# Issue order at a decoder block's two layer norms and at the joining of its seven-product banks

## The chip, the core and the metric

The kernel runs on one core of one Trainium2 chip. The time is the device time of one launch in microseconds (us). TensorE (PE in the profile; its weight loads are PEld) multiplies, VectorE (DVE) and ScalarE (ACT) do elementwise work, GpSimd (POOL) does very little and issues a few DMAs, SyncE (SP) issues the other DMAs. Lower is better.

## What is computed

One decoder block on 256 tokens of width 2048, in float32. Only its second half touches the change:

```python
mix = token_mixers(x, ...)                # ends in merged @ w_out
x = layer_norm(ALPHA * x + mix, ln1_g, ln1_b)
h = gelu(causal_dwconv(x @ w_gate, conv_w, conv_b)) * (x @ w_up)
x = layer_norm(ALPHA * x + h @ w_down, ln2_g, ln2_b)
x = x + sigmoid(x @ w_ple_gate) * (p @ w_ple_proj)
```

`w_out` and `w_ple_gate` are 2048 x 2048, `w_gate` and `w_up` 2048 x 5632, `w_down` 5632 x 2048, `w_ple_proj` 256 x 2048.

## The kernel before

**Split operands.** Each float32 operand is split into a rounded part `hi` and the rest `lo`; a product is hi times hi, hi times lo and lo times hi. Tokens form two halves, t = 0 and 1, of 128.

**Units.** Weights come in 284 units of 128 x 2048, used in a fixed order: 120 to 135 are `w_out`, 136 to 223 alternate gate and up, 224 to 267 are `w_down` (22 for each half of its output columns), 268 to 283 the last gate. `unit()` (line 179) hands out the next unit and first calls `prep()` (line 158) until the units up to two ahead are prepared. A prep, for each half h of the unit, loads `raw` by SyncE's queue (a ring of four half-unit tiles), copies it to `hi` on ScalarE (line 170, the helper of line 107) and subtracts on VectorE for `lo` (line 171). The `hi` and `lo` tiles are six each, that is three units.

**Order of the work.** The program is traced in Python order; a scheduler then orders each engine's instructions by priority and readiness in its own model of time. `tc.high_priority(n)` raises the priority of what is traced in it. `tc.keep_in_program_order(ins)` pins an instruction behind the one traced last before it on the same engine (an order of issue, with no semaphore). `tc.manual_schedule(engines=...)` keeps an engine to the traced order. SyncE is under it all along; TensorE only in `end1`.

**The down projection and its joining.** `residual()` (line 921) runs the residual projections in two halves of output columns through `x_half()` (line 324). Most units are multiplied directly into four PSUM banks. Some units of the down projection (`DNW`; nine in the first half, eight in the second) use seven products in place of eight, in `seven()` (line 284). Four of these go to extra banks p1, p5, p7 and p6; after the last such unit `joined()` (line 937) adds them to the residual `z`: ScalarE copies p1 to `ju` (line 107), VectorE does `z = ALPHA * z + p1` (line 943) and then a chain of additions (lines 943 and 948). All have the priority `P_STAT`, the highest.

**First layer norm (`end1`, line 1020).** TensorE's order is by hand: the last two units of `w_out` for token half 0 and then 1 (`tail_mm`; each call is six matmuls of 512 columns), mixed with the projection of `p` (`proj(k, t)`, six matmuls; its results go through `put`, a ScalarE copy and a store by GpSimd's queue), with turns, and with the first three gate and up units. `stat` makes mean and scale; `norm(g)` normalizes one of four blocks of 512 columns, on VectorE (lines 889 and 891) for g of 0 and 2 and on ScalarE (line 894) for the others; `turn(g)` transposes that block by four matmuls of 128 columns into one of two `mx` banks (line 901), from which the engines make `x1T`: for g of 1 and 3 in four pieces `lny` by turns on ScalarE and VectorE (lines 911 and 913), then a hi copy and a subtraction (line 916). `LN_ORDER` takes the blocks as 1, 0, 3, 2. `phase0(i)` multiplies unit 136 + i with token half 0 (16 matmuls of 256 columns, line 250), which needs only `hi` parts; `phase1(j)` does half 1 and all `lo` parts of the three units in four slices.

**Second layer norm (`ln_out`, line 836).** It does the same steps into `x2T`, called by `done2` for each token half when its columns are done; before half 1, `ple_proj` traces 24 matmuls of the projection. Here the scheduler orders TensorE too. Norms are on VectorE for g = 0 (line 849), else on ScalarE (line 852); transposes are line 855, the four pieces of each block lines 862 and 864, the subtraction 867. The following `x_half` for the gate starts with two units whose matmuls are traced for t = 0 and then for t = 1 (12 matmuls a unit and half).

Of the kernel before, what the change touches and what calls it, by code (L numbers as in the profile page):

```python
# [9 lines left out]
F32 = mybir.dt.float32  # L10
# [36 lines left out]
DNW = (DNP, DNP[:-1])  # L47
WH = 1152
# [7 lines left out]
def tile_block(ctx: ExitStack, tc: tile.TileContext, wu, wfv, wpp, xT_in, x_in, pT_in, wlr,  # L56
# [66 lines left out]
    sums, half = {}, {}  # L123
# [34 lines left out]
    def prep():  # L158
# [6 lines left out]
        for h in range(2):  # L165
# [5 lines left out]
            nc.vector.tensor_tensor(lo, raw, hi.bitcast(F32), ALU.subtract)  # L171
# [7 lines left out]
    def unit():  # L179
        u = n_used[0]  # L180
        n_used[0] += 1
        while n_prep[0] < min(NU, u + 3):
            prep()
        for v in (u, u + 1):
            if v in half:
                split_seven(v)
        return ready.pop(u)
# [136 lines left out]
    def x_half(name, act, K, evac, pulls=0, head=0, tail=0, mid=None, done=None, end=None,  # L324
               fine=False, ws=(), joined=None):
# [15 lines left out]
        for t in range(2):  # L341
            for i, w in enumerate(us):
                mm(i, w, (t,))
# [492 lines left out]
    def ln_out(zs, stats, t, act_out, cg, cb, nm, prio):  # L836
# [3 lines left out]
        with tc.high_priority(P_STAT):  # L840
            nc.vector.bn_aggr(mv[:, 0:2], stats[t])
            nc.vector.tensor_scalar(mv[:, 2:3], mv[:, 1:2], LN_EPS, None, ALU.add)
            nc.gpsimd.tensor_tensor(mv[:, 3:4], mv[:, 2:3], mhalf, ALU.pow)
            nc.vector.tensor_scalar(mv[:, 4:5], mv[:, 0:1], -1.0, mv[:, 3:4], ALU.mult, ALU.mult)
        with tc.high_priority(prio):
            for g in range(4):
                zc = z[:, g * 512:g * 512 + 512]
# [3 lines left out]
                else:  # L851
                    nc.scalar.activation(zc, zc, AF.Identity, scale=mv[:, 3:4], bias=mv[:, 4:5])
                pt = mxtile(f"pt{nm}{t}{g}")
# [15 lines left out]

    def ln_steps(zs, stats, t, act_out, gb_, cg, cb, nm):  # L870
# [13 lines left out]
        def norm(g):  # L884
            e = slice(g * 512, g * 512 + 512)
            zc = z[:, e]
            with tc.high_priority(P_LN1[t]):
                if g in AFF_DVE:
                    nc.vector.scalar_tensor_tensor(zc, zc, mv[:, 0:1], gb_[0][:, e],
                                                   ALU.subtract, ALU.mult)  # L890
                    nc.vector.scalar_tensor_tensor(zc, zc, mv[:, 3:4], gb_[1][:, e],
                                                   ALU.mult, ALU.add)
                else:
                    nc.scalar.activation(zc, zc, AF.Identity, scale=mv[:, 3:4], bias=mv[:, 4:5])
# [26 lines left out]
    def residual(name, act, K, zs, stats, mid, done=None, end=None, ws=((), ())):  # L921

        for nh in range(2):
# [13 lines left out]
            def joined(ms, zp=zp):  # L937
# [12 lines left out]
                with tc.high_priority(P_STAT):  # L950
                    copy(u, p1)

                onto(0, 0, p1)
# [47 lines left out]
    def ple_proj(half, w, pTs):  # L1001
        banks = [[[mmtile(f"pp{half}{t}{c}")] for c in range(2)] for t in range(2)]
        for k in range(2):
            o = slice(k * 1024, k * 1024 + 1024)
# [307 lines left out]
```

## Time and profile before

| | us |
|---|---|
| median of 3 runs | 1664.32 (1663.75 to 1664.76) |
| the profiled execution | 1663.05 |
| its span, first to last instruction | 1661.3 |
| TensorE busy with matmuls | 1650.9 |
| VectorE busy | 1193.2 |
| ScalarE busy | 865.4 |

Matmuls are pipelined, and the profile models their ends: a matmul's shown duration overlaps the next one's. Where TensorE's time matters, distances from start to start are read. A bracket at the end of a timeline row is the engine's idle time before it and what ended it. Line numbers (L171) are those of the kernel before. Arrows read out <- in, by the program's tile names with numbers left out, so `hi<-raw` stands for every unit.

### The profile page before, as it was taken

To read this page: it belongs to the slowest core of one execution; us is meant where nothing else is said; L and a number is where in the kernel's file an instruction comes from. 1 tells how busy PE (TensorE), PEld (TensorE's weight loads), DVE (VectorE), ACT (ScalarE), POOL (GpSimd) and SP (SyncE) were. 2 spreads that over 40 slices of the span, in tenths; PEclk is the share of its full clock that TensorE was granted. 3 is DMA by queue.
4 is the path that set the end of the run, shared out by engine and by line. 5 is a ranking of instruction groups with operands and counts; after the bars stand their busy time and mean duration, and the time that the engine had idled before them with its cause. 6 is when DMAs were issued, how large, how long until landed. Compare 5 with 4: busy or idle time off the path is not lost.

```text
span 1661.3 us, 24083 instructions
## 1 busy us (share of the span) xinstructions
PE 1650.9 (99%) x8984; PEld 1432.3 (86%) x8984; DVE 1193.2 (72%) x1751; ACT 865.4 (52%) x1245; POOL 62.8 (4%) x175
## 2 busy tenths in 40 slices
PE   9999999999999999999999999999999999999998
PEld 8988888888888888888888888888888888888787
DVE  6666658768756657775677777777777788887874
ACT  6745445445555544544465555555555555454733
POOL 0000000000000000000010000000000011010000
PEclk9999999999999999999999999999999999999999
DMA  7665555555555555667746666666666667695554
GB/s 295 232 201 183 165 188 181 177 179 177 184 178 174 173 189 194 194 195 283 235 150 209 231 232 205 206 211 205 205 209 205 202 246 271 223 345 208 183 192 168
DMA packets 95588, 343.87 MB, mean 207 GB/s; under 512 B 11064, under 2 KB 12736, under 8 KB 94064
## 3 DMA queue, kind: packets, MB, share of 16 engines
q1 hardware_dynamic: 90528, 324.51, 58.3%
q0 software_dynamic: 4944, 17.84, 2.8%
q8 instruction: 70, 1.15, 0.3%
q14 instruction: 46, 0.38, 0.1%
HBM read 332.33 MB, written 9.97 MB: 206 GB/s over the span
## 4 chain that ended last, share of the span: by engine, by line
PE 94%; DVE 2%; DMA 2%; ACT 1%; issue 1%; SPq 0%; POOL 0%; DVEq 0%; ACTq 0%
PE psu L237 9%; PE psg L237 9%; PE psm L237 7%; PE dn L281 7%; PE gr L281 5%; PE gv L281 5%; PE wo L281 5%; PE psu L239 5%; PE psg L239 5%; PE pg L281 4%; PE psm L239 4%; PE psa L237 3%; PE fv L426 2%; PE psfq L237 2%; PE psfk L237 2%; PE psq L237 2%
## 5 line engine op out<-in xcount | busy, mean ns | idle before, releaser
L107 ACT ACTIVATE hi<-raw 128x1024 fp32r<-128x1024 f32 (+1 forms) x568 | 593.0, 1047 | 629.2 <-issue 217.0
L171 DVE TENSOR_TENSOR lo<-raw,hi 128x1024 fp32r<-128x1024 f32 x534 | 653.1, 1225 | 358.1 <-ACT hi L107 357.1
L237 PE MATMUL psu<-x1T,hi 128*128 128x512 f32 x688 | 236.0, 389 | 0.0
L237 PE MATMUL psg<-x1T,hi 128*128 128x512 f32 x672 | 230.5, 389 | 0.0
L239 PE MATMUL psu<-x1T,lo 128*128 128x256 f32 x688 | 190.0, 276 | 0.0
L239 PE MATMUL psg<-x1T,lo 128*128 128x256 f32 x672 | 185.5, 276 | 0.0
L237 PE MATMUL psm<-xT,hi 128*128 128x512 f32 x512 | 175.8, 391 | 0.0
L237 PEld LDWEIGHTS psu<-x1T,hi 128*128 128x128 f32 x688 | 129.2, 188 | 26.7
L237 PEld LDWEIGHTS psg<-x1T,hi 128*128 128x128 f32 x672 | 126.2, 188 | 26.1
L239 PE MATMUL psm<-xT,lo 128*128 128x256 f32 x512 | 141.5, 276 | 0.0
L239 PEld LDWEIGHTS psu<-x1T,lo 128*128 128x128 f32 x688 | 129.1, 188 | 0.0
L239 PEld LDWEIGHTS psg<-x1T,lo 128*128 128x128 f32 x672 | 126.2, 188 | 0.0
L281 PE MATMUL dn<-hi,hT 128*128 128x512 f32 x432 | 121.4, 389 | 0.0
L237 PEld LDWEIGHTS psm<-xT,hi 128*128 128x128 f32 x512 | 96.2, 188 | 19.8
L239 PEld LDWEIGHTS psm<-xT,lo 128*128 128x128 f32 x512 | 96.2, 188 | 0.1
L281 PEld LDWEIGHTS dn<-hi,hT 128*128 128x128 f32 x432 | 81.0, 188 | 16.8 <-ACT hi L107 0.2
L237 PE MATMUL psa<-oT,hi 128*128 128x512 f32 x256 | 87.8, 389 | 0.0
L281 PE MATMUL gv<-hi,xT 128*128 128x512 f32 x256 | 72.3, 394 | 0.0
L281 PE MATMUL gr<-hi,xT 128*128 128x512 f32 x256 | 72.2, 394 | 0.0
L239 PE MATMUL psa<-oT,lo 128*128 128x256 f32 x256 | 70.7, 276 | 0.0
L281 PE MATMUL wo<-hi,mT 128*128 128x512 f32 x256 | 70.2, 390 | 0.0
L281 PE MATMUL dn<-lo,hT 128*128 128x512 f32 x216 | 68.9, 391 | 0.6 <-DVE lo L171 0.5
(300 smaller groups left out, 2806.2 us busy)
## 6 DMA issues: line engine op xcount, KB each, us to landing
raw<-in_wu_dram SPq DMA_DIRECT2D x568, 512.0 KB, 4.7
fvraw<-in_wfv_dram SPq DMA_DIRECT2D x14, 524.0 KB, 7.9
hi<-hsd POOLq DMA_DIRECT2D x17, 256.0 KB, 5.1
lo<-hsd POOLq DMA_DIRECT2D x17, 256.0 KB, 5.3
lnb<-in_lng_dram SPq DMA_DIRECT2D x4, 1024.0 KB, 9.0
hsd<-hsh POOLq DMA_DIRECT2D x9, 256.0 KB, 5.7
hsd<-hsl POOLq DMA_DIRECT2D x9, 256.0 KB, 5.5
z<-in_x_dram SPq DMA_DIRECT2D x2, 1024.0 KB, 8.5
```

The costliest lines, as they stand in the source:

```text
L107: nc.scalar.activation(o, i, AF.Copy, bias=0.0, scale=scale)
L171: nc.vector.tensor_tensor(lo, raw, hi.bitcast(F32), ALU.subtract)
L237: nc.tensor.matmul(ps, lhsT=hi[i // 8 if hoff == 0 else 0][:, w0 % 1024:w0 % 1024 + P], rhs=a[:, kt % 4, :], start=first and i == 0, stop= ...
L239: nc.tensor.matmul(ps[:, 256:512], lhsT=lo[i // 8 if hoff == 0 else 0][:, w0 % 1024:w0 % 1024 + P], rhs=a[:, kt % 4, 0:256], start=False, ...
L281: nc.tensor.matmul(bs[j][:, 0:m], lhsT=x, rhs=v[:, o:o + m], start=first and i == 0, stop=last and i == 2)
L426: nc.tensor.matmul(fbk[t][c][:, 0:n], lhsT=x, rhs=w[:, o:o + n], start=kt == 0 and i == 0, stop=kt == 15 and i == 2)
```

## The change

It alters the order in which instructions are issued.

- **Joining:** ScalarE's copy of p1 and VectorE's first addition are pinned behind what was traced before them on their engines; the last of this are hi copies and lo subtractions of the two units already asked for.
- **First border:** all four groups of `tail_mm` for half 1 come before the first turn, and the projection's groups shift between the turns. Half 1's norms, the projection's copies and the lo parts of units 137 and 138 (`LATE_LO`) are pinned behind half 0's last turn and then placed one by one between half 1's turns. `unit(3 - i)` asks for no further units in these phases.
- **Second border:** `ln_out` becomes `ln_parts`, which gives the same three steps as functions, and TensorE's order is written out from the last two dn units (`end2`) to the first two units of the gate (`begin3`). The lo parts of units 270 and 271 (`PIN_LO`) are pinned behind what was traced before them on VectorE.

```diff
@@ -45,6 +45,8 @@
 DNW = (DNP, DNP[:-1])
+LATE_LO = (137, 138)
+PIN_LO = (270, 271)
 WH = 1152
@@ -120,7 +122,7 @@
-    sums, half = {}, {}
+    sums, half, later = {}, {}, {}
@@ -168,7 +170,16 @@
             lo = w_tile("lo", F32R, f"lo{u}_{h}", u)
-            nc.vector.tensor_tensor(lo, raw, hi.bitcast(F32), ALU.subtract)
+            def rest(lo=lo, raw=raw, hi=hi):
+                return nc.vector.tensor_tensor(lo, raw, hi.bitcast(F32), ALU.subtract)
+            if u in LATE_LO:
+                later.setdefault(u, []).append(rest)
+            elif u in PIN_LO:
+                tc.keep_in_program_order(rest())
+            else:
+                rest()
             his.append(hi)
@@ -176,10 +187,10 @@
-    def unit():
+    def unit(ahead=3):
         u = n_used[0]
         n_used[0] += 1
-        while n_prep[0] < min(NU, u + 3):
+        while n_prep[0] < min(NU, u + ahead):
             prep()
@@ -322,7 +333,7 @@
     def x_half(name, act, K, evac, pulls=0, head=0, tail=0, mid=None, done=None, end=None,
-               fine=False, ws=(), joined=None):
+               fine=False, ws=(), joined=None, begin=None):
@@ -338,9 +349,12 @@
         us = [unit() for _ in range(head)]
-        for t in range(2):
-            for i, w in enumerate(us):
-                mm(i, w, (t,))
+        if begin is not None:
+            begin(lambda i, t: mm(i, us[i], (t,)))
+        else:
+            for t in range(2):
+                for i, w in enumerate(us):
+                    mm(i, w, (t,))
         for i in range(head, n - tail):
@@ -833,23 +847,31 @@
-    def ln_out(zs, stats, t, act_out, cg, cb, nm, prio):
+    def ln_parts(zs, stats, t, act_out, cg, cb, nm, prio):
...
         mv = sm.tile([P, 8], F32, tag="mv", name="mv")
-        with tc.high_priority(P_STAT):
-            nc.vector.bn_aggr(mv[:, 0:2], stats[t])
-            nc.vector.tensor_scalar(mv[:, 2:3], mv[:, 1:2], LN_EPS, None, ALU.add)
-            nc.gpsimd.tensor_tensor(mv[:, 3:4], mv[:, 2:3], mhalf, ALU.pow)
-            nc.vector.tensor_scalar(mv[:, 4:5], mv[:, 0:1], -1.0, mv[:, 3:4], ALU.mult, ALU.mult)
-        with tc.high_priority(prio):
-            for g in range(4):
-                zc = z[:, g * 512:g * 512 + 512]
+        def stat():
+            with tc.high_priority(P_STAT):
+                nc.vector.bn_aggr(mv[:, 0:2], stats[t])
+                nc.vector.tensor_scalar(mv[:, 2:3], mv[:, 1:2], LN_EPS, None, ALU.add)
+                nc.gpsimd.tensor_tensor(mv[:, 3:4], mv[:, 2:3], mhalf, ALU.pow)
+                nc.vector.tensor_scalar(mv[:, 4:5], mv[:, 0:1], -1.0, mv[:, 3:4],
+                                        ALU.mult, ALU.mult)
+        def norm(g):
+            zc = z[:, g * 512:g * 512 + 512]
+            with tc.high_priority(prio):
                 if g in ZN_DVE:
...
                     nc.scalar.activation(zc, zc, AF.Identity, scale=mv[:, 3:4], bias=mv[:, 4:5])
+        def turn(g):
+            zc = z[:, g * 512:g * 512 + 512]
+            with tc.high_priority(prio):
                 pt = mxtile(f"pt{nm}{t}{g}")
@@ -867,6 +889,8 @@
+        return stat, norm, turn
     def ln_steps(zs, stats, t, act_out, gb_, cg, cb, nm):
@@ -881,17 +905,18 @@
-        def norm(g):
+        def norm(g, keep=lambda ins: None):
             e = slice(g * 512, g * 512 + 512)
...
                 if g in AFF_DVE:
-                    nc.vector.scalar_tensor_tensor(zc, zc, mv[:, 0:1], gb_[0][:, e],
-                                                   ALU.subtract, ALU.mult)
+                    keep(nc.vector.scalar_tensor_tensor(zc, zc, mv[:, 0:1], gb_[0][:, e],
+                                                        ALU.subtract, ALU.mult))
                     nc.vector.scalar_tensor_tensor(zc, zc, mv[:, 3:4], gb_[1][:, e],
...
                 else:
-                    nc.scalar.activation(zc, zc, AF.Identity, scale=mv[:, 3:4], bias=mv[:, 4:5])
+                    keep(nc.scalar.activation(zc, zc, AF.Identity, scale=mv[:, 3:4],
+                                              bias=mv[:, 4:5]))
@@ -948,9 +973,10 @@
                 with tc.high_priority(P_STAT):
-                    copy(u, p1)
-                onto(0, 0, p1)
+                    tc.keep_in_program_order(nc.scalar.activation(u, p1, AF.Copy, bias=0.0,
+                                                                  scale=1.0))
+                    tc.keep_in_program_order(nc.vector.scalar_tensor_tensor(
+                        zp(0, 0), zp(0, 0), ALPHA, p1, ALU.mult, ALU.add))
                 plus(u, u, p6)
@@ -998,13 +1024,6 @@
-    def ple_proj(half, w, pTs):
-        banks = [[[mmtile(f"pp{half}{t}{c}")] for c in range(2)] for t in range(2)]
-        for k in range(2):
-            o = slice(k * 1024, k * 1024 + 1024)
-            x_mm(banks, (w[0][:, o], w[1][:, o]), pTs[k], (0, 1), k == 0, k == 1)
-        return banks
     z1 = [s8([P, 2048], name=f"z1{t}") for t in range(2)]
@@ -1033,13 +1052,14 @@
                     o = t2("ppo")
-                    copy(o, pb[t][c][0])
+                    tc.keep_in_program_order(nc.scalar.activation(
+                        o, pb[t][c][0], AF.Copy, bias=0.0, scale=1.0))
                     nc.gpsimd.dma_start(ppd[t, :, c * 512:c * 512 + 512], o)
...
             def phase0(i):
-                us.append(unit())
+                us.append(unit(3 - i))
                 ps.append(mmtile(("psg0", "psu0", "psg1")[i]))
@@ -1056,31 +1076,43 @@
                 norm0(g)
-            for i in range(2):
-                tail_mm(1, 0, i)
-            tail_mm(1, 1, 0)
+            for c in range(2):
+                for i in range(2):
+                    tail_mm(1, c, i)
             turn0(G[0])
-            tail_mm(1, 1, 1)
+            proj(0, 0)
             turn0(G[1])
...
                 norm0(g)
-            proj(0, 0)
+            proj(1, 0)
             turn0(G[2])
-            proj(1, 0)
-            put(0)
-            for g in G[:2]:
-                norm1(g)
             proj(0, 1)
             turn0(G[3])
+            keep = tc.keep_in_program_order
+            u1, u2 = LATE_LO
+            def low(u, i):
+                with tc.high_priority(P_LN1[1]):
+                    keep(later[u][i]())
+            norm1(G[0], keep)
+            norm1(G[1], keep)
+            put(0)
+            low(u1, 0)
+            norm1(G[2], keep)
             proj(1, 1)
             put(1)
-            for i in range(3):
-                phase0(i)
-                turn1(G[i])
-                if i == 0:
-                    for g in G[2:]:
-                        norm1(g)
+            phase0(0)
+            turn1(G[0])
+            low(u2, 0)
+            norm1(G[3], keep)
+            phase0(1)
+            turn1(G[1])
+            low(u1, 1)
+            phase0(2)
+            turn1(G[2])
+            low(u2, 1)
             for j in range(4):
@@ -1180,12 +1212,56 @@
-    def done2(t):
-        if t == 1:
-            pb.extend(ple_proj(1, *pq[0]))
-        ln_out(z2, st2, t, x2T, c_g2, c_b2, "l2", P_LN2[t])
-    residual("dn", hT, NF, z2, st2, ({14: lambda: mid2(0), 15: lambda: mid2(1)}, {8: mid2a, NF // 2 - 5: mid2b}), done2, ws=DNW)
+    late_turns = []
+    border = ExitStack()
+    def end2(tail_mm):
+        border.enter_context(tc.manual_schedule(engines={mybir.EngineType.PE}))
+        stat0, norm0, turn0 = ln_parts(z2, st2, 0, x2T, c_g2, c_b2, "l2", P_LN2[0])
+        stat1, norm1, turn1 = ln_parts(z2, st2, 1, x2T, c_g2, c_b2, "l2", P_LN2[1])
+        late_turns.append(turn1)
+        for c in range(2):
+            for i in range(2):
+                tail_mm(0, c, i)
+        stat0()
+        for g in range(4):
+            norm0(g)
+        for c in range(2):
+            for i in range(2):
+                tail_mm(1, c, i)
+        stat1()
+        w, pTs = pq[0]
+        pb.extend([[mmtile(f"pp1{t}{c}")] for c in range(2)] for t in range(2))
+        def proj(k, t):
+            o = slice(k * 1024, k * 1024 + 1024)
+            x_mm(pb, (w[0][:, o], w[1][:, o]), pTs[k], (t,), k == 0, k == 1)
+        proj(0, 0)
+        proj(0, 1)
+        for g in range(4):
+            norm1(g)
+        turn0(0)
+        proj(1, 0)
+        turn0(1)
+        proj(1, 1)
+        turn0(2)
+        turn0(3)
+    def begin3(mm):
+        turn1, = late_turns
+        mm(0, 0)
+        turn1(0)
+        mm(1, 0)
+        turn1(1)
+        mm(0, 1)
+        turn1(2)
+        mm(1, 1)
+        turn1(3)
+        border.close()
+    residual("dn", hT, NF, z2, st2, ({14: lambda: mid2(0), 15: lambda: mid2(1)}, {8: mid2a, NF // 2 - 5: mid2b}), end=end2, ws=DNW)
     pp = [s8([P, 2, 1024], name=f"ppk{i}") for i in range(2)]
@@ -1213,7 +1289,7 @@
                tail=2 if nh == 1 else 0, mid={4: mid3} if nh == 0 else None,
-               fine=nh == 1)
+               fine=nh == 1, begin=begin3 if nh == 0 else None)
     assert n_used[0] == NU, (n_used[0], NU)
```

## The prediction

> **What bounds the kernel now.** I read the totals first, then the granted clock, then who TensorE waits for.
>
> ```profile
> PE 1650.9 (99%) x8984; PEld 1432.3 (86%) x8984; DVE 1193.2 (72%) x1751; ACT 865.4 (52%) x1245; POOL 62.8 (4%) x175
> ```
> ```profile
> core 0: 1661.3 us, clock 1.000
> ```
> ```profile
> ...
> PE psg L250 <- DVE x1T L916: 1.1, 1, 1.1
> PE ptl L855 <- DVE z L849: 0.9, 1, 0.9
> PE dn L281 <- DVE lo L171: 0.5, 1, 0.5
> PE pg L281 <- DVE lo L171: 0.3, 1, 0.3
> PE dn1m L302 <- DVE ts L154: 0.2, 1, 0.2
> ```
>
> TensorE is the bound, at a full clock, and beside two waits at the kernel's start these are all that the waits view gives it (total, times, longest, in us). The first three (first layer norm, second layer norm, end of the down projection) lie where the diff edits. No change of order can give more than what TensorE loses there, so the first step is to measure that loss properly. A wait in this view is counted from the modelled end of the matmul before, which overlaps its successor; the true loss is the distance between starts, less the undisturbed distance. That comes from the chain of waits:
>
> ```profile
> 1344.15 5.44 PE dn L281 x24
> ```
>
> 24 matmuls of 512 columns in 5.44 us are 0.227 us each; 256 columns take half. Now TensorE's rows around the three places, in the timeline (start, duration, what, count):
>
> ```profile
> 836.48 0.39 PE L281 MATMUL wo<-hi,mT 128*128 128x512 f32 x1
> 836.95 0.66 PE L901 MATMUL ptl<-ident,z 128*128 128x128 f32 x4
> ...
> 845.76 1.07 PE L250 MATMUL psg<-x1T,hi 128*128 128x256 f32 x8
> 847.96 1.35 PE L250 MATMUL psg<-x1T,hi 128*128 128x256 f32 x8 [1.13 <-DVE x1T L916]
> 849.14 0.60 PE L901 MATMUL ptl<-ident,z 128*128 128x128 f32 x4
> ...
> 1547.00 0.61 PE L281 MATMUL dn<-hi,hT 128*128 128x512 f32 x2
> 1547.66 0.50 PE L281 MATMUL dn<-lo,hT 128*128 128x512 f32 x1
> 1548.00 0.86 PE L281 MATMUL dn<-hi,hT 128*128 128x512 f32 x3
> 1549.38 0.50 PE L281 MATMUL dn<-lo,hT 128*128 128x512 f32 x1 [0.53 <-DVE lo L171]
> 1549.72 0.39 PE L281 MATMUL dn<-hi,hT 128*128 128x512 f32 x1
> ...
> 1557.00 0.62 PE L281 MATMUL dn<-hi,hT 128*128 128x512 f32 x2
> 1558.48 1.09 PE L855 MATMUL ptl<-ident,z 128*128 128x128 f32 x8 [0.87 <-DVE z L849]
> 1559.33 0.47 PE L281 MATMUL dn<-lo,hT 128*128 128x512 f32 x1
> ```
>
> First border: 836.95 - 836.48 - 0.23 = 0.24; 847.96 - 845.76 - 8 x 0.113 = 1.29; the eight after it take 1.18 and not 0.91, 0.27. Together 1.80. End of the down projection: 0.21 before 1547.66, 0.11 after it (a restart), 0.70 before 1549.38, 0.11 after it: 1.13. Second border: 1558.48 - 1557.00 - 0.45 = 1.03. **All three: 3.96 us**, 0.24% of the time. That is the ceiling of the main argument.
>
> **The change part by part.** It neither adds nor removes arithmetic: the same matmuls, transposes (64 in 16 turns of four), norms, lo subtractions and DMAs, on the same engines. Only issue order changes, so each part is worth the lost time above that it removes, less what it makes late.
>
> *Joining.* These rows of ScalarE, VectorE and then the last lo subtraction of the down projection show why TensorE was late at 1549:
>
> ```profile
> 1525.59 0.60 ACT L107 ACTIVATE ju<-dn1m 128x512 f32<-128x512 f32 x1 [8.12 <-PE dn1m L302]
> 1526.08 3.89 ACT L107 ACTIVATE hi<-raw 128x1024 fp32r<-128x1024 f32 x4
> 1526.22 0.69 DVE L943 SCALAR_TENSOR_TENSOR z<-z,dn1m 128x512 f32<-128x512 f32 x1 [7.49 <-ACT ju L107]
> ...
> 1548.11 1.23 DVE L171 TENSOR_TENSOR lo<-raw,hi 128x1024 fp32r<-128x1024 f32 x1 [0.50 <-ACT hi L107]
> ```
>
> The first joining instruction was queued ahead of four hi copies, stood 8.12 us waiting for TensorE's last seven-product bank, and with it VectorE for 7.49 us; then everything came at once, and the lo parts ran behind until 1549.38. The pin puts the copy behind the hi parts, and the first z addition behind the lo parts, of the two units already asked for. How much earlier these run is not shown: at least 0, if their hi tiles (six, three units) are still held by TensorE; at most 8.12. The missed amount at 1549 is 0.70, so one microsecond is enough. I take it as enough, since the idle is eight times that: -1.13; the other end is 0. The joining itself starts up to one copy (1.0) later; nothing waits for it before the evacuations 24 us further on. In half 0 nothing stood idle; I count 0.
>
> *First border.* These rows lie between the third turn's transposes and the release of the long stall:
>
> ```profile
> 840.69 0.66 PE L901 MATMUL ptl<-ident,z 128*128 128x128 f32 x4
> 841.15 1.21 DVE L171 TENSOR_TENSOR lo<-raw,hi 128x1024 fp32r<-128x1024 f32 x1
> 844.25 1.41 DVE L889 SCALAR_TENSOR_TENSOR z<-z,mv,lnb 128x512 f32<-128x512 f32 x2
> 845.57 0.41 DVE L913 TENSOR_SCALAR lny<-ptl,chn 128x128 f32<-128x128 f32 x1
> 845.89 1.41 DVE L891 SCALAR_TENSOR_TENSOR z<-z,mv,lnb 128x512 f32<-128x512 f32 x2
> 847.21 0.69 DVE L916 TENSOR_TENSOR x1T<-lny,x1T 128x512 fp32r<-128x512 f32 x1
> ```
>
> From 840.69 to 847.90 half 0's transposed block x1T took 7.21 us, of which 1.21 + 2 x 1.41 = 4.03 of VectorE were another's work: a lo part and half 1's norm. That is now pinned behind half 0's last turn, and so are half 1's norm and the projection's copies on ScalarE. TensorE also finishes the residual's four last matmul groups ahead of the first transposes, which removes the 0.24. That moves the third turn later by one group of six, 1.36, while phase 0 starts about where it did. The block is then ready about 4.0 - 1.4 = 2.6 earlier against a stall of 1.29; I leave 0.1 for the block behind it. **-1.7.** What is moved is due later: the lo parts of units 137 and 138 in phase 1, three phase-0 stretches of 16 x 0.113 = 1.8 away. They hold four raw buffers longer, so unit 139's load waits on SyncE's queue, behind which only later loads stand; the projection's stores on GpSimd's queue move by some microseconds too, with nothing urgent behind them. Its copies free a bank for the third phase-0 stretch, two stretches and two turns (4.5 us) later.
>
> ```profile
> raw<-in_wu_dram SPq DMA_DIRECT2D x568, 512.0 KB, 4.7
> ```
>
> Released at about 849 and 4.7 in flight, that load lands at 854; unit 139's hi tile is free only when TensorE has gone through half of phase 1, about 856. Hidden; without this cover it would cost its lateness one for one.
>
> *Second border.* TensorE's order is now written out. The first transposes came before the last two dn matmuls and the projection, and had to wait 1.03 for a norm; now they follow 24 residual matmuls of token half 1 and 12 of the projection, 36 x 0.227 = 8.2 us after token half 0 ends. Here are half 0's last evacuation in the trace, and one turn from its transposes to the last read of its bank:
>
> ```profile
> 1554.59 0.68 DVE L932 TENSOR_TENSOR z<-z,dn 128x512 f32<-128x512 f32 x1
> 1564.21 0.60 PE L855 MATMUL ptl<-ident,z 128*128 128x128 f32 x4
> 1567.20 0.47 ACT L862 ACTIVATE lny<-ptl,chn 128x128 f32<-128x128 f32 x1
> ```
>
> The old transposes began 3.9 after 1554.59, so 8.2 is cover enough: -1.03. The new order has a narrow place of its own: turn 3 directly follows turn 2, and there are two banks, so it needs turn 1's bank. By the written order it comes 0.45 (a turn) + 1.36 (six projection matmuls) + 0.45 = 2.26 after turn 1. A turn occupies its bank for r: 0.60 and four pieces of 0.41 and 0.47 by turns are at least 2.36; the row gives 1567.67 - 1564.21 = 3.46, with half 1's statistics and norms between the pieces. Now these are mostly done by then, so I take 2.8, nearer the pieces: +0.5. From 2.36 to 3.46 it is 0.1 to 1.2. Pinning lo parts of units 270 and 271 costs nothing: unit 270 is due 48 x 0.227 = 10.9 us after turn 3.
>
> [...]
>
> **Sum:** -1.13 - 1.7 - 1.03 + 0.5 = -3.4. On the profiled span 1661.3 becomes 1657.9; that execution took 1663.05, 1.3 below the median of the runs. On the median, 1664.3 - 3.4 = **1660.9**.
>
> **The rivals.**
> 1. *More is gained* (0.18). The two last waits of the view (0.3, 0.2) are 0.5 idle; the down projection's 0.5 stood for 1.13 lost, so an estimate of about 1.1 is lost there. If VectorE's earlier lo parts take that along: 1659.8. Against: neither place is edited.
> 2. *The bank becomes the wait* (0.13). With r between 3.46 and the 5.3 of the first border's third turn (840.69 to 845.98), say 4.4, turn 3 waits 2.1: 1664.3 - 3.9 + 2.1 = 1662.5; at 5.3, 1663.8.
> 3. *The pin doesn't do what it says* (0.10): hi tiles of the two units are freed so late that the copies can't run before the joining; the 1.13 stays, 1662.0.
> 4. *Slower* (0.07). One mechanism: the written order lets TensorE do nothing else while a turn waits. Turn 3 waits r - 2.26. Turns 0 and 2 of half 0 and the first of half 1 share the other bank, 3.62 apart as written (two turns of 0.45 and 12 matmuls of 0.227), so once r is over 2 x 3.62 - 2.26 = 4.98 that lane adds r - 4.98, together 2r - 7.24. The gain of 3.9 is used up at r = 5.6. At the 7.21 of the first border's block it is 7.2, and 0.9 more at half 1's third turn (written 6.34 after its first): 1664.3 - 3.9 + 8.1 = 1668.5. For it: r was already 5.3 in one turn. Against: that one had the work in it that is now pinned away, and the other row has 3.46.
>
> [...]
>
> **How the numbers follow.** Forecast 0.52, rivals 0.18, 0.13, 0.10, 0.07. A measurement of this kernel tells about 0.2%, 3.3 us, from no change: the line is at 1661.0. The forecast's residue of 0.1 to 1.2 puts it between 1660.5 and 1661.6, about three fifths of its chance under the line, since I take r near 2.8: 0.32, with rival 1, 0.50 faster. Rivals 2 and 3 and the rest of the forecast, 0.43, are no change. Slower 0.07. The range goes from rival 1 with some room, 1659.5, to 1663.4 in rival 2.
>
> **What would show it.** In the waits view, psg <- x1T, ptl <- z and dn <- lo are gone or under 0.3. The joining's copy follows hi copies, and VectorE's 7.49 idle is broken up by lo parts. On TensorE, tail groups, then projection, then transposes. A wait of ptl for a lny piece is the residue; over 1.5 it is rival 2. The sum is wrong if TensorE stalls at a new place, in unit 267, half 1's turns, or behind 139.

## The result, and the profile after

| | us |
|---|---|
| before, 12 executions beside the changed kernel | median 1663.86 (1662.34 to 1664.9) |
| after, 12 executions | median 1667.07 (1664.43 to 1670.0) |
| ratio | 1.0022, 95% interval 1.0014 to 1.0030 |
| profiled execution after, its span | 1666.08, 1664.3 |

The change makes the kernel 3.2 us slower; forecast were 3.4 us less. Totals, clock and TensorE's waits (total, times, longest) of the changed kernel:

```profile
PE 1652.1 (99%) x8984; PEld 1433.0 (86%) x8984; DVE 1193.4 (72%) x1751; ACT 866.4 (52%) x1245; POOL 62.8 (4%) x175
```
```profile
core 0: 1664.3 us, clock 0.999
```
```profile
PE ptl L877 <- ACT lny L884: 1.9, 1, 1.9
...
PE dn L292 <- ACT hi L109: 0.9, 1, 0.9
PE dn L292 <- DVE lo L175: 0.8, 1, 0.8
PE ptl L926 <- DVE z L915: 0.6, 1, 0.6
PE psg L261 <- DVE x1T L941: 0.6, 1, 0.6
PE dn1m L313 <- DVE ts L156: 0.5, 1, 0.5
PE ptl L926 <- DVE x1T L799: 0.2, 1, 0.2
```

(L877, 884, 886 are the second border's transposes and pieces; L926, 915, 941 the first border's transposes, second norm operation and last subtraction; L109 and L175 make hi and lo.) The 1.1 of the first border and the 0.9 of the second are gone, and seven waits stand where there were five. TensorE's rows at the down projection's end and at the second border:

```profile
1547.64 0.40 PE L292 MATMUL dn<-hi,hT 128*128 128x512 f32 x1
1548.97 0.49 PE L292 MATMUL dn<-hi,hT 128*128 128x512 f32 x1 [0.93 <-ACT hi L109]
1550.23 0.57 PE L292 MATMUL dn<-lo,hT 128*128 128x512 f32 x1 [0.77 <-DVE lo L175]
1550.59 1.05 PE L292 MATMUL dn<-hi,hT 128*128 128x512 f32 x2
1551.44 0.63 PE L292 MATMUL dn<-lo,hT 128*128 128x512 f32 x1
...
1565.12 0.60 PE L877 MATMUL ptl<-ident,z 128*128 128x128 f32 x4
1565.47 1.64 PE L292 MATMUL pp<-pw,pTs 128*128 128x512 f32 x6
1566.95 0.60 PE L877 MATMUL ptl<-ident,z 128*128 128x128 f32 x4
1569.45 0.66 PE L877 MATMUL ptl<-ident,z 128*128 128x128 f32 x4 [1.90 <-ACT lny L884]
```

Unit 267 now costs two waits, 1548.97 - 1547.64 - 0.23 = 1.10 and 1.03. Behind them matmuls of 512 columns take (1551.44 - 1550.59) / 2 = 0.425 us in place of 0.227, until 1554: 1.57 lost. The windows view gives the reason, its column after POOL's being the granted clock:

```profile
1546.00:1550.40 4.40, 2.71 (x11) 1.51 (x10) 2.45 (x2) 1.06 (x1) 0.00 (x0) 1.00 0.87 208
1550.40:1553.80 3.40, 3.40 (x9) 2.66 (x10) 2.08 (x3) 2.12 (x2) 0.00 (x0) 0.52 0.89 343
```

TensorE is busy throughout the second stretch, at half the clock (0.52, since the first 0.12 us of it are still at full clock). Further on, half 0's turn 3 waits 2.12 from start to start for the bank of turn 1 (1565.12).

Here is what TensorE loses in five stretches, as in the prediction: distances from start to start less the undisturbed ones, summed. About 2.0 in the fourth is there without any wait: a turn's four transposes take 1565.12 - 1563.29 - 1.36 = 0.47 in the changed kernel, and 0.23 is counted as undisturbed, an estimate by columns from the 0.227 of 512. e3, e15 and e16 are experiments below.

| us from the span's start | before | after | e3 | e15 | e16 |
|---|---|---|---|---|---|
| 830 to 870, first border | 4.13 | 4.52 | 4.06 | 4.49 | 4.52 |
| 1400 to 1535, joining | 0.41 | 0.58 | 0.58 | 0.52 | 0.29 |
| 1535 to 1556.5, units 266 and 267 | 1.12 | 3.98 | 1.16 | 2.02 | 2.54 |
| 1556.5 to 1590, second border | 3.06 | 4.05 | 5.99 | 2.13 | 2.02 |
| 1590 to 1655, end | 1.33 | 0.67 | 1.26 | 0.87 | 1.13 |
| sum | 10.05 | 13.80 | 13.05 | 10.03 | 10.50 |

After less before is 3.75; the two spans differ by 3.0, and the other 0.7 was gained in the first 172 us, which the change doesn't touch. So none of the three parts gained, and the loss is at units 266 and 267 and in the second border.

**Where the first border's gain went.** VectorE's rows there:

```profile
851.99 1.22 DVE L175 TENSOR_TENSOR lo<-raw,hi 128x1024 fp32r<-128x1024 f32 x1
853.13 0.75 DVE L913 SCALAR_TENSOR_TENSOR z<-z,mv,lnb 128x512 f32<-128x512 f32 x1
853.79 1.22 DVE L175 TENSOR_TENSOR lo<-raw,hi 128x1024 fp32r<-128x1024 f32 x1
854.92 0.74 DVE L915 SCALAR_TENSOR_TENSOR z<-z,mv,lnb 128x512 f32<-128x512 f32 x1
```

Two of the moved lo parts stand ahead of the two operations of half 1's last norm; its second ends at 854.92 + 0.74 = 855.66, and the turn that needs it was due at 855.05. The old stall of 1.29 became three of 0.38, 0.77 and 0.72, at half 0's last turn, half 1's last turn and the x1T made from that.

**Where the joining's gain went.** The pin does what it says, but VectorE goes on to wait for the last seven-product bank in the next joining instruction:

```profile
1525.81 0.58 ACT L976 ACTIVATE ju<-dn1m 128x512 f32<-128x512 f32 x1
```
```profile
1533.48 0.69 DVE L973 TENSOR_TENSOR ju<-ju,dn1m 128x512 f32<-128x512 f32 x1 [6.08 <-PE dn1m L313]
```

The copy waits no longer, after hi copies; VectorE's 7.49 idle became 6.08, one instruction on. The seven operations that VectorE did between 1526.8 and 1533.7 before now run from 1518.5 to 1527.4, and then it has nothing to do until the bank comes. The same addition started at 1533.71 before, without a wait, so little time was won.

Further back than VectorE, what makes unit 267's last parts late is a load. These are the hi copies that the last lo parts are made with, before and after:

```profile
1547.01 1.06 ACT L107 ACTIVATE hi<-raw 128x1024 fp32r<-128x1024 f32 x1 [1.10 <-DMA raw<-in_wu_dram]
```
```profile
1547.86 1.06 ACT L109 ACTIVATE hi<-raw 128x1024 fp32r<-128x1024 f32 x1 [1.87 <-DMA raw<-in_wu_dram]
```

Both wait for a load. Its `raw` buffer was last used for the projection's weights, and SyncE issues the load right behind the VectorE subtraction that frees it: at 1541.76 behind a subtraction that ends at 1541.73 before, at 1542.93 behind one that ends at 1542.91 after. In the new order more of the joining's chain stands ahead of that subtraction.

### The profile page after: what moved, and what is told of

It is laid out like the page before. It is cut to its first block, busy times and chain, and to the rows that moved or that the text cites. A ratio compares the mean times of both kernels' runs of the same rounds, so it can differ in the third digit from the quotient of the medians.

```text
span 1664.3 us, 24082 instructions
## 1 busy us (share of the span) xinstructions
PE 1652.1 (99%) x8984; PEld 1433.0 (86%) x8984; DVE 1193.4 (72%) x1751; ACT 866.4 (52%) x1245; POOL 62.8 (4%) x175
## 4 chain that ended last, share of the span: by engine, by line
PE 94%; DVE 2%; ACT 1%; DMA 1%; issue 1%; SPq 0%; POOLq 0%; POOL 0%; DVEq 0%; ACTq 0%
PE psu L248 9%; PE psg L248 9%; PE dn L292 7%; PE psm L248 7%; PE gr L292 5%; PE gv L292 5%; PE wo L292 5%; PE pg L292 5%; PE psu L250 5%; PE psg L250 5%; PE psm L250 4%; PE psa L248 3%; PE fv L440 2%; PE dn L313 2%; PE psq L248 2%; PE psfq L248 2%
## 5 line engine op out<-in xcount | busy, mean ns | idle before, releaser
L109 ACT ACTIVATE hi<-raw 128x1024 fp32r<-128x1024 f32 (+1 forms) x568 | 592.7, 1047 | 640.5 <-issue 221.6
L175 DVE TENSOR_TENSOR lo<-raw,hi 128x1024 fp32r<-128x1024 f32 x534 | 652.2, 1223 | 357.4 <-ACT hi L109 356.5
```

The source lines that it names most:

```text
L109: nc.scalar.activation(o, i, AF.Copy, bias=0.0, scale=scale)
L175: return nc.vector.tensor_tensor(lo, raw, hi.bitcast(F32), ALU.subtract)
```

## The experiments

Each was timed in five rounds, beside the kernel before on the same chip (medians of before: 1663.59 for e1 to e4, 1663.62 for e5 to e9, 1664.09 for e11 to e14, 1663.38 for e15 to e18, 1664.22 for e19 and e20).

**The parts one by one: e1 to e4.** Theory A: the written second border asks for unit 267 too early. Theory B: the pinned joining makes 267's parts late. The edits, shortened, are the diff's own parts, put into the kernel before, and the changed kernel without the pin:

```diff
 e1, on the kernel before
-                    copy(u, p1)
-                onto(0, 0, p1)
+                    tc.keep_in_program_order(nc.scalar.activation(u, p1, ...))
+                    tc.keep_in_program_order(nc.vector.scalar_tensor_tensor(zp(0, 0), ...))
 e2, on the kernel before: LATE_LO, unit(3 - i), end1 as changed
 e3, on the kernel before: PIN_LO, ln_parts, end2, begin3
 e4, on the kernel after: the lines of e1 the other way round
```

> The joining pinned, both borders as before. Theory A (TensorE's written order asks for unit 267 too early, and that is what costs): the scheduler may still put unit 266's matmuls first, so the pin alone changes little, 1663 to 1664.5, with VectorE's long idle moved from the first addition to the wait for the bank p6. Theory B (the pin itself makes the lo parts of 266 and 267 late): the stalls before 1550 are as long as in the changed kernel, over 2 us with the slow stretch behind them, and the time is 1666 to 1667. The prediction's step: the 1.13 us there vanish, 1662.7.

> Only the first border changed (order, pinned norms, late lo parts of 137 and 138). Theory A: as the changed kernel's trace has it, about 2.1 us of new stalls (0.48 at the fourth turn, 0.85 at half 1's last turn, 0.83 in phase 1) for the 1.8 us removed: 1664.2, within 0.5 of before. The prediction's step would give 1662.2.

> Only the second border changed (TensorE's written order from unit 266 on, lo parts of 270 and 271 pinned), the joining as before. Theory A: unit 267's parts are no earlier than before (lo at about 1549), and the written order needs them after six matmuls of the last stretch: 1.5 to 2.5 us of stalls there, a slow stretch behind them in most executions, and the wait of turn 3 of about 2: 1666 to 1668, mean clock 0.998 to 0.999. Theory B: no long stall before 1550, only turn 3's wait against the 1.03 removed: 1664.9, clock 1.000.

> The changed kernel with the joining as before. Theory A: no better than the changed kernel, 1666 to 1668, clock 0.998 to 0.999. Theory B: the stalls before 1550 shrink to the 1.1 of before, 1664.5 to 1665.3, clock 1.000.

| | median | ratio to before |
|---|---|---|
| e1, joining | 1662.89 | 0.9997 (0.9988 to 1.0006) |
| e2, first border | 1663.14 | 0.9997 (0.9988 to 1.0005) |
| e3, second border | 1666.40 | 1.0019 (1.0010 to 1.0028) |
| e4, after without joining | 1666.58 | 1.0020 (1.0011 to 1.0028) |

The second border alone makes 2.8 of the 3.2 us. B falls as the cause of the loss. A explains little: 267's waits are 0.49 and 0.45 in e3, together as long as before, and the loss is turn 3's. TensorE in e3:

```profile
1562.35 0.60 PE L877 MATMUL ptl<-ident,z 128*128 128x128 f32 x4
1562.70 1.64 PE L292 MATMUL pp<-pw,pTs 128*128 128x512 f32 x6
1564.24 0.66 PE L877 MATMUL ptl<-ident,z 128*128 128x128 f32 x4
1567.00 0.66 PE L877 MATMUL ptl<-ident,z 128*128 128x128 f32 x4 [2.11 <-ACT lny L884]
1567.41 0.71 PE L292 MATMUL pg<-hi,x2T 128*128 128x512 f32 x2
1567.96 1.01 PE L292 MATMUL pg<-lo,x2T 128*128 128x512 f32 x2
1568.77 1.91 PE L292 MATMUL pg<-hi,x2T 128*128 128x512 f32 x4
```

Turn 3 waits 2.32 from start to start, and soon after it four matmuls take 1570.47 - 1568.77 = 1.70 in place of 0.91: the half-speed stretch, here in the border. New theories: C, ScalarE's queue holds the bank (half 1's norms stand between the pieces); D, the written distance from turn 1 to turn 3 is too short; F, the half-speed stretch comes from TensorE's idle time.

**Distance, queue, unit 267, idle time: e5, e6, e7, e9.** All in `end2`, shortened; e9 on e3, the others on the changed kernel:

```diff
 e5
-        proj(0, 0); proj(0, 1); norm1(0..3); turn0(0); proj(1, 0); turn0(1); proj(1, 1); turn0(2); turn0(3)
+        proj(0, 0); norm1(0..3); turn0(0); proj(0, 1); turn0(1); proj(1, 0); turn0(2); proj(1, 1); turn0(3)
 e6
+        norm1(1..3), pinned, behind turn0(1)
 e7, tail_mm(0, c, i)
-        for c in range(2): for i in range(2):
+        for i in range(2): for c in range(2):
 e9, on e3
         proj(1, 1); turn0(2)
+        proj(1, 1)
         turn0(3)
```

> The changed kernel with half 0's four turns of the second border spread evenly among the projection's four parts: projection, turn 0, projection, turn 1, projection, turn 2, projection, turn 3. From turn 1's transposes to turn 3's there are then two parts of the projection, about 3.66 us by the rows at 1563.29 and 1565.12 of the profile after (1.83 us for a turn and a part), in place of about 2.2. Theory D (the written distance is shorter than the 4.2 us in which a bank is emptied, and the wait for it is the loss): turn 3 waits about 0.5 us in place of 2.1, a stretch of matmuls at 0.427 us behind it goes, and the time falls by 1.5 to 3 us, to 1664 to 1665.5. Theory A (unit 267 is asked for too early, and the border's order is innocent): no change, 1666.5 to 1667. Theory C (ScalarE's queue holds the bank, whatever the distance): the bank comes as much later as the distance grows, no change.

> The changed kernel with half 1's three ScalarE norms of the second border pinned behind the evictions of half 0's turn 1 (two of the three move behind them in ScalarE's order). Theory C (the norms, 0.66 us each, stand between the four pieces by which a turn's bank is emptied): turn 3 waits 0.7 to 1.4 us less than the 2.1 us after, and the time falls by 0.7 to 3 us (the larger figure if a stretch of matmuls at 0.427 us goes with it), to 1664 to 1666.3. Theory D (the distance alone): no more than 0.3 us is gained. Half 1's own turns come 3 us later than these norms and should not wait more than 0.3 us.

> The changed kernel with the down tail's half 0 written by unit, not by bank: unit 266 into both banks, then unit 267 into both, so that 267 is due 2.7 us into the tail in place of 1.36 us. Theory A (unit 267 asked for too early): its two waits, 1.1 and 1.03 us in the profile after, lose 1.36 us together, with the stretch at 0.427 us behind them, and the time falls by 1 to 2.5 us, to 1664.5 to 1666. Theory D: no change in the time but for these waits, since turn 3's wait stays at about 2.1; with a mean over executions in which the waits of 267 are 0.9 to 1.1 together, as in two of the three other kernels with this order, 0.5 to 0.9 us.

> The kernel before with the second border's order alone (as in the run with the second border alone), and between half 0's turns 2 and 3 six matmuls of 128x512 more, 1.36 us: the last part of the projection is added a second time, so the output holds that part twice. Theory F (the stretch of seven or eight matmuls at 0.427 us in place of 0.227 comes from TensorE's idle time ahead of it, and costs 1.4 to 1.6 us): the wait for turn 3's bank falls from 2.3 to about 0.95 us with work in its place, the slow stretch goes or shrinks, and with 1.36 us more of work the time is 0.5 to 1.6 us shorter than the 1666.40 of the kernel without the filling: 1664.8 to 1665.9. Rival (the slow stretch has another cause, or waits are refilled for nothing): the same time, within 0.4 us; second rival (the bank is held by a chain that moves along with the matmuls): 1.36 us longer, 1667.8.

| | median | ratio to before |
|---|---|---|
| e5, turns spread | 1664.01 | 1.0003 (0.9995 to 1.0012) |
| e6, half 1's norms later | 1665.02 | 1.0005 (0.9997 to 1.0014) |
| e7, unit 267 due later | 1666.42 | 1.0016 (1.0006 to 1.0025) |
| e9, six matmuls more | 1665.49 | 1.0010 (1.0001 to 1.0019) |

The waits at the border in e5, e6 and e9, one fence each:

```profile
1565.96 0.65 PE L877 MATMUL ptl<-ident,z 128*128 128x128 f32 x4 [1.42 <-ACT lny L884]
```
```profile
1569.53 0.66 PE L878 MATMUL ptl<-ident,z 128*128 128x128 f32 x4 [1.23 <-ACT lny L885]
```
```profile
1567.62 0.66 PE L877 MATMUL ptl<-ident,z 128*128 128x128 f32 x4 [1.50 <-ACT lny L884]
1570.38 0.66 PE L877 MATMUL ptl<-ident,z 128*128 128x128 f32 x4 [0.73 <-ACT lny L884]
```

e5 gets most of the loss back, but not as D had it: a wait of 1.59 stays, now at turn 2, so the bank is late by itself and not only asked for early. e6 takes 0.67 off turn 3's wait, and C is part of it. e7 cuts unit 267's waits from 2.13 to 0.55, and then turns 2 and 3 wait 1.50 and 1.47 for their banks, since two of half 1's norms stand on ScalarE ahead of its second piece of turn 0, and a half-speed stretch follows. The gain is given back; A was no more than a part. e9, whose output holds one part of the projection twice, does 1.36 us more work than e3, has no half-speed stretch in its profile and is not slower than e3 by ratio. That speaks for F, but not by the sum of the waits: e9's are longer (1.67 and 0.89, now at turns 2 and 3) than e3's 2.32. The last section sets these waits beside the others.

**What holds a bank: e11, e12, e14.** The changed kernel's VectorE, GpSimd and ScalarE behind turn 0's transposes (which start at 1563.29):

```profile
1562.89 1.22 DVE L175 TENSOR_TENSOR lo<-raw,hi 128x1024 fp32r<-128x1024 f32 x1
1564.56 0.21 DVE L860 TENSOR_SCALAR mv<-mv 128x1 f32<-128x1 f32 x1 [0.45 <-POOL mv L859]
1564.69 0.40 DVE L886 TENSOR_SCALAR lny<-ptl,chn 128x128 f32<-128x128 f32 x1
```
```profile
1562.93 1.59 POOL L859 TENSOR_TENSOR mv<-mv,mhalf 128x1 f32<-128x1 f32 x1 [5.06 <-DVE mv L858]
```
```profile
1565.12 0.46 ACT L884 ACTIVATE lny<-ptl,chn 128x128 f32<-128x128 f32 x1 [0.37 <-DVE lny L886]
1565.48 0.81 ACT L870 ACTIVATE z<-z,mv 128x512 f32<-128x512 f32 x1
```

Turn 0's first piece stands on VectorE behind half 1's statistics (L860), which wait for GpSimd; that is theory G. ScalarE's first piece waits for VectorE's, then a norm of half 1 comes between. e11 pins L860 and VectorE's norm of half 1 behind turn 1, e12 begins and spreads the turns as well, e14 is e12's second border on the kernel before (both shortened):

```diff
 e11
+        shift1(pinned); norm1(0..3, pinned on VectorE)      # behind turn0(1)
 e12, e14
+        turn0(0); proj(0, 0); turn0(1); shift1(pinned); norm1(0..3); proj(0, 1); turn0(2); proj(1, 0); turn0(3); proj(1, 1)
```

> The changed kernel, its written order on TensorE untouched, with the two VectorE operations of half 1's second norm that wait for GpSimd's power (the shift, line 860, and the norm of its fourth quarter, line 867) pinned behind half 0's turn 1. Theory G (it is VectorE's queue that makes the bank late: in the profile after, turn 0's first piece waits from 1563.9 to 1564.69 behind line 860, which waits for a power of 1.59 us at 1562.93, and ScalarE's norms then start between the pieces): the bank of turn 1 is emptied 2.8 to 3.3 us after its transposes in place of 4.2, turn 3 waits 0.6 to 1.2 us in place of 2.1 to 2.3, and the time falls by 1 to 3 us (the larger figure where a stretch at 0.427 us goes too): 1664 to 1666. Theory D (the distance of turns alone, whatever stands in the queues): 1666.5 to 1667.

> The same, and the written order spread and begun earlier: turn 0 straight behind the down tail, then a part of the projection behind each turn, the last part behind turn 3. Theories D and G together: turns 1 to 3 are then 3.66 us apart two by two against 2.8 to 3.3 us for a bank, the wait of 2.1 goes and none over 0.5 us takes its place in the border; unit 267's waits of 0.9 to 2.1 us stay. 1663.3 to 1664.7, that is level with the kernel before or 0.5 us over it. Rival (turn 0 then waits for half 0's norm, whose ScalarE part ends at 1560.4 where the tail ends at 1560.6): up to 1 us more.

> The kernel before with this second border alone, spread and begun earlier, with the pinned operations; first border and joining as before. If the written order itself was sound and only its distances and queues were wrong, the 1.03 to 1.7 us that TensorE waits ahead of the second border in the kernel before go, and 0.2 to 0.5 us come back at unit 267: 1662.2 to 1663.3 against 1663.6, the first version faster than before. If the written order costs as such, 1664 to 1665.

| | median | ratio to before |
|---|---|---|
| e11 | 1665.36 | 1.0008 (0.9999 to 1.0016) |
| e12 | 1664.85 | 1.0005 (0.9996 to 1.0014) |
| e14 | 1664.81 | 1.0000 (0.9991 to 1.0009) |

G falls short. In e11 turn 3 still waits 1.76, in e12 and e14 turn 2 waits 1.27 and 1.19. VectorE and ScalarE in e11 show what is left:

```profile
1564.40 0.41 DVE L889 TENSOR_SCALAR lny<-ptl,chn 128x128 f32<-128x128 f32 x1
1565.34 0.73 DVE L889 TENSOR_SCALAR lny<-ptl,chn 128x128 f32<-128x128 f32 x2 [0.53 <-ACT lny L887]
```
```profile
1564.85 0.46 ACT L887 ACTIVATE lny<-ptl,chn 128x128 f32<-128x128 f32 x1 [0.39 <-DVE lny L889]
1565.79 0.46 ACT L887 ACTIVATE lny<-ptl,chn 128x128 f32<-128x128 f32 x1 [0.48 <-DVE lny L889]
```

The four pieces of a turn go strictly in turn, 1564.40, 1564.85, 1565.34, 1565.79, each engine waiting for the other's piece. Whatever stands in either queue holds the bank, and the engine that waits holds its own queue. That is theory H.

**One engine for a whole bank: e15 to e18.** In `ln_parts` (e18: `ln_out` of the kernel before), on the changed kernel, on e12, on e14 and on the kernel before:

```diff
-                    if i % 2:
+                    if g % 2 == 0:
                         nc.scalar.activation(y[:, i, :], src, AF.Identity, scale=gc, bias=bc)
```

> The changed kernel, with the four pieces of a turn of the second border all on one engine: even quarters on ScalarE, odd ones on VectorE, in place of every second piece on the other engine. Theory H (the pieces of one bank by two engines go one after another, each waiting for the other engine's queue, so that whatever stands in either queue holds both banks): turn 0's pieces start at once on ScalarE and turn 1's on VectorE behind line 860; a bank is emptied 1.8 to 2.4 us after its transposes in place of 4.2, turn 3 waits under 0.6 us in place of 2.1, and the time falls by 1.7 to 3.2 us: 1663.9 to 1665.4. Theory D alone (a bank takes as long by one engine as by two): turn 3's wait stays over 1.5 us, 1666 to 1667.

> The changed kernel with all three edits of the second border: turns spread and begun straight behind the tail, half 1's late operations pinned behind turn 1, one engine for a turn. By theories D, G and H no wait over 0.4 us is left in the border but that of turn 0 for half 0's norm (up to 1 us). Unit 267's two waits, 0.9 to 2.1 us, stay. 1663 to 1664.3, against 1664.85 without the one engine for a turn; if H falls, 1664.5 to 1665.

> The kernel before with this second border alone, all three edits; first border and joining as before. Against 1664.81 without the one engine for a turn, whose profile has a wait of 1.19 us at turn 2: that wait goes, 1663.3 to 1664.2, and 1662.5 if what turn 0 waits goes too, which would be the first version faster than before (about 1663.8).

> The kernel before with one engine for a turn in the second border, and nothing else. Its turns wait for no bank now (its stall of 1.03 us is ahead of turn 0), so by theory H nothing is to be had: 1663.3 to 1664.3. If it is faster by more than 0.8 us, the gain of the other three is not the written order's.

| | median | ratio to before |
|---|---|---|
| e15, on after | 1663.96 | 1.0006 (0.9997 to 1.0015) |
| e16, on e12 | 1662.97 | 0.9996 (0.9987 to 1.0005) |
| e17, on e14 | 1662.91 | 0.9998 (0.9989 to 1.0007) |
| e18, on before | 1663.24 | 0.9995 (0.9986 to 1.0004) |

ScalarE's, VectorE's and TensorE's rows in e15, whose written order is that of the changed kernel:

```profile
1562.60 1.47 ACT L884 ACTIVATE lny<-ptl,chn 128x128 f32<-128x128 f32 x4
```
```profile
1563.70 1.37 DVE L886 TENSOR_SCALAR lny<-ptl,chn 128x128 f32<-128x128 f32 x4
```
```profile
1563.06 0.60 PE L877 MATMUL ptl<-ident,z 128*128 128x128 f32 x4
1564.89 1.03 PE L877 MATMUL ptl<-ident,z 128*128 128x128 f32 x8
```

Two banks are emptied side by side, turn 1's within 1565.07 - 1563.06 = 2.0 us in place of 4.3, and turns 2 and 3 run as one group of eight transposes: no wait in the border at all. H holds. In e16 and e17 no turn waits for a bank either; over e12 and e14 they gain 1.5 and 0.3 us by ratio, which lies within the intervals. On the kernel before, where no turn waits for a bank, the edit is worth nothing that can be measured, as expected. No version is measurably faster than the kernel before; e16 and e17 are level with it.

**The first border and the pin once more: e19 and e20.** On e16; in e20 the joining's pin goes too:

```diff
-            low(u2, 0)
             norm1(G[3], keep)      # both operations pinned
+            low(u2, 0)
```

> The changed kernel with the three edits of the second border, and in the first border half 1's fourth norm, both its VectorE operations, pinned ahead of the pinned lo part of unit 138 in place of behind it. Theory P (the pinned lo parts of 1.22 us each stand between that norm's two operations and make half 1's last turn and its x1T late): the two waits of 0.76 and 0.71 us go, 1.3 to 1.5 us less than 1662.97: 1661.5 to 1662, clearly under the kernel before (about 1663.6). Rival (the wait moves on to the tail of half 1's last quarter, which ScalarE's table load of 1.28 us holds anyway): 0.3 to 0.8 us less, 1662.2 to 1662.7.

> The same without the pinned joining. Theory B in its smaller form (the pin makes unit 267 about 0.9 us later where the second border asks for it in a written order): unit 267's waits are 0.9 to 1.5 us in place of about 2.0, and the time is 0.5 to 1 us less than that of the run beside it: 1660.7 to 1661.5. If the pin is innocent: the same within 0.4 us.

The medians, 1664.81 and 1664.21 (ratios 1.0033, 1.0008 to 1.0058, and 1.0026, 1.0003 to 1.0048), say little: nine of the 24 executions took 1676.2 to 1679.1 us and the rest 1662.5 to 1665.5. The profiled ones (1664.52 and 1663.09) are not of the nine, so what adds 14 us there stays open. None of e16's 11 executions has it. In e19's first border the waits only moved:

```profile
856.77 0.39 PE L265 MATMUL psg<-x1T,lo 128*128 128x256 f32 x1 [0.33 <-DVE lo L175]
862.01 0.39 PE L261 MATMUL psg<-x1T,hi 128*128 128x256 f32 x1 [0.90 <-DVE x1T L944]
```

The norm is in time; now a lo part is late (0.49 from start to start), and the last x1T waits 1.07. In e20 unit 267's waits are 1.19 together, 2.00 in e19: the pin seems to cost 0.8 there, which the times don't resolve.

## Why the prediction was wrong

- **Joining, "one microsecond is enough" (-1.13): failed.** The copy moved as meant, but the idle time was not the copy's; it was the wait for the last bank, and the chain's next addition took it over (6.08 of 7.49). Nor was it VectorE's backlog that made the lo part late at 1549: the row shown for it, with its 0.50 behind an hi copy, was misread. That copy waited 1.10 for its load, and the load goes out 1.17 later after the change. The pin alone makes it as late (1543.24 in e1), but in the scheduler's own order TensorE lost no more there (0.8 against 1.1), and e1 changes nothing measurable. In the changed kernel unit 267's parts are later, not earlier: 2.13 of waits against 0.90. Profiles without the pin have 0.9 to 1.5 (e3, e4, e9, e14, e17, e20); those with pin and written border, at the same tail order, 1.9 to 2.3, but e5 1.03. That the parts are late by the pin together with the written border is read from profiles only.
- **First border (-1.7): failed at "What is moved is due later".** The check was made for the lo parts against phase 1, and not for half 1's norm in the same stretch of VectorE's time. 1.87 of new waits took the place of 1.80 (e2: no change in time; e19: the waits move again).
- **Second border (-1.03 + 0.5): the old stall went, as forecast, and turn 3 waited for its bank, as forecast; r was mis-sized.** I took 2.8, since half 1's statistics and norms are "mostly done by then". They came right there, and r was 1569.45 - 1565.12 = 4.33: rival 2 with nearly the r that it named, 4.4, and a wait of 2.12 against its 2.1. The engines' strict turns made r long (e15: 2.0 by one engine).
- **r's lower end, 2.36, took the four pieces one after another.** No run shows that they have to go so. In e11's turn they did: the pieces end at 1564.81, 1565.31 and 1565.75, and the next start at 1564.85, 1565.34 and 1565.79. It meant more than that: the two engines didn't work on the bank side by side there, each waited for the other's piece (0.39, 0.53, 0.48), and that coupled their queues.
- **Rival 2's price, 1662.5, was too low too**, since it kept the gains at the other two places and had no half speed in it. *Slower* was given 0.07 with another mechanism (r over 5.6); it came from r = 4.3 with the other gains absent.
- **Not in the prediction at all: half speed.** 1.57 us in the profiled execution, of 3.0 in all.

## What to carry to other kernels

A stall that is moved is gained only if the next instruction in the same queue isn't waiting for the same thing, and if everything traced behind it was checked against its own due time. Before an order is written out by hand, measure how long a buffer is held in that order, with what will then stand in the queues that empty it. Where two engines empty one bank by turns, each inherits the other's queue (here a bank took 4.33 us); a bank each lets them run side by side (2.0 in e15). And follow a late operand back to its load before a busy or idle engine is blamed for it.

## What the runs showed of the hardware

TensorE's clock was halved for 3.4 us at a time in the middle of the kernel, 1.4 to 1.6 us lost each time. In e3 the same windows view has, around turn 3's wait and behind it:

```profile
1564.60:1568.01 3.41, 1.30 (x10) 0.98 (x9) 2.01 (x5) 3.38 (x8) 0.00 (x0) 1.00 0.01 5
1568.01:1571.42 3.41, 3.41 (x10) 2.67 (x9) 2.42 (x5) 3.38 (x8) 0.00 (x0) 0.50 0.00 0
1571.42:1574.84 3.42, 3.42 (x19) 2.80 (x18) 2.36 (x4) 1.64 (x4) 0.00 (x0) 1.00 0.00 0
```

The wait itself and the first us behind it are at full clock, the busy stretch after them is at half, and then the full clock is back. Between 1540 and 1580 us six profiles have such a stretch, with matmuls of 512 columns 0.425 us apart, and in each TensorE had just waited 2.1 to 3.4 us within 5 us: 1.10 + 1.03 (after), 2.32 (e3), 1.02 + 2.32 (e4), 1.24 + 1.03 (e6), 1.50 + 1.47 (e7), 1.22 + 1.03 (e12). Profiles with less show none there (1.59 in e5, 1.68 in e1, 1.92 in e11, 2.00 in e19). But three others have none either: e16 with 1.30 + 1.03, e9 with 1.67 + 0.89, and the changed kernel behind its own 2.12. So waits of 2.1 us or more stand ahead of all six, and such waits alone were not enough.

What else decides is not shown. The clock in the traces gives one hint. In the changed kernel's it is recorded as full from 4.284, half from 1550.522 for 3.413 us, full again, and half from 1663.161 to the end. In lengths of that stretch, the two changes to half lie 453.0 and 486.0 behind 4.284; in the kernel before, full from 4.167 and half from 1659.630, it is 485.0. If the changed kernel's execution is cut into spans of 3.413 us from 4.284 on, the span just ahead of 1550.522 holds both waits, 2.13 in all; of turn 3's 2.12, behind which the clock stayed full, 1.9 lie in one span. This is a reading of two profiles, and no experiment moved a wait across the end of a span.

The mean granted clock gives a hint for executions without a trace. 3.4 us at half clock lower a mean over 1664 us by 0.001. The mean also counts half speed behind the last matmul, where it costs nothing: in the kernel before it is 1.00 up to 1659.60 and 0.51 from there to 1661.30, without a matmul, which lowers that mean by 0.0005. So the figure of one execution is no count of stretches. The changed kernel's 12 executions have 1.000 once, 0.999 seven times, 0.998 three times and 0.997 once, mean 0.9987; the kernel before beside e5 has a mean of 0.9996 (22 times 1.000, 8 times 0.999, twice 0.998). If the end weighs the same in both, that is about one stretch more in each execution, an estimate of 1.6 of the 3.2 us. The times go with it: in e7 four executions at 1.000 took 1663.9 to 1665.2 us, and five at 0.998 took 1667.3 to 1669.3. With six matmuls put into the wait (e9), 9 of 11 executions have 1.000, against 4 of 11 in e3.
